# Opening of a two-layer decoder trunk: first transfers on two queues, written order of the first splits, two accumulations interleaved, one spread placed

## The chip, the cores and the metric

The kernel runs on one core of one Trainium2 chip, as a single program. The metric is the device time of that program in microseconds (us); the time of a kernel is the median of its runs.

The core has five engines that matter here. TensorE (PE in the profile) multiplies matrices into PSUM; VectorE (DVE), ScalarE (ACT) and GpSimd (POOL) work elementwise; SyncE (SP) issues transfers, and ScalarE can issue transfers too. Each engine executes its own instructions strictly in the order in which they stand in its queue. The transfers themselves run on 16 DMA engines.

## The reference

The input is one sequence of 512 tokens with 1024 features, in float32. Two layers follow one another; each has a mixer (layer 0 a causal Conformer convolution module, layer 1 differential attention), a SwiGLU feed-forward part and a gated per-layer embedding. The change touches only the beginning of layer 0:

```python
u = rms_norm(h, conv_norm_g)            # h = x
a = u @ w_pw1 + b_pw1                   # 1024 -> 2048
u = a[..., :D] * sigmoid(a[..., D:])    # gated half
u = depthwise_conv(u, 31 taps) + dw_b
u = silu(layer_norm(u))
h = h + (u @ w_pw2 + b_pw2)
```

`rms_norm` multiplies each token by one over the root of the mean of its squares, and each feature by a gain.

## The kernel before

**Layout.** Features lie on the 128 partitions and tokens along the free axis, so h is eight chunks h[0] to h[7] of 128 x 512. The weight w_pw1 comes in tiles of 128 x 1024, one for each 128 output features: its eight blocks of 128 x 128 are the stationary operands for the eight chunks of the input.

**Products in three parts.** Float32 products are made of three faster ones. Each operand is split into a high part, rounded to the type fp32r, and a low part, what the rounding left. For a weight, ScalarE casts the high part (L159) and VectorE subtracts (L161). For a chunk of the norm, `Norm.split` has ScalarE multiply h[c] by the gain and round (L206), and VectorE form the low part (L207). The gain is a column of a small table `vec`, which is loaded by a transfer of its own (L120). `mm3` then issues low x high (L166), high x high (L167) and high x low (L168). The text calls each of these 128x512 instructions a product.

**The norm is applied late.** The per-token factor is not applied to the input. It is worked out beside the products and multiplied into their result. `columns_of_chunks` squares every h chunk on ScalarE (L237); the squares of chunks 0 to 2 go one by one into a sum over features on TensorE (`columns_sum`, L199, short passes of 128 columns against a matrix of ones), those of chunks 3 to 7 are first added on GpSimd (L241) and then summed. VectorE (L270) and GpSimd (L272) make the inverse root, VectorE spreads it on a diagonal (L277), and `spread` multiplies this by ones on TensorE (L288), so that every partition holds the factor of every token. ScalarE copies that to SBUF as `rb` (L262).

**The conv stage.** The loop over c (L500) makes output chunk c: `half(wg)` and `half(wa)`, 24 products each (eight input chunks times three), fill two PSUM tiles; VectorE multiplies both by `rb` (L523, L529), ScalarE takes the sigmoid (L524), VectorE multiplies the two (L533 or L541). The convolution of a finished chunk is done in one of two ways. For chunks 0, 2, 4 and 7 most taps are run on VectorE (L453 to L458) and some on ScalarE and GpSimd (L445, L446); chunk 7 also has eight on TensorE (L363). The chunks in `PHASED` (1, 3, 5, 6) go through DRAM and come back in another layout (`phased_in`, L370 and L374), are convolved on TensorE with banded matrices (L407), and go back the same way (L417, L420). Weights of chunk c + 1 are loaded and split while chunk c is made, in two raw buffers (tag `wraw`): a load waits until the raw tile two loads ahead of it has been split.

**What sets the order.** The Tile framework's planner simulates the kernel when it is built and writes each engine's queue. It prefers what stands earlier in the program among the instructions that its simulation finds ready. `tc.issue_after(x)` adds an edge: what is issued in the block stands behind x on its engine. `tc.manual_schedule(engines=...)` keeps the written order on the named engines.

**The opening before.** SP issues the two halves of the first weight, h[0], the halves of the second weight, and the other chunks of h, in an order that alternates between them (L155, L297); ScalarE's queue issues `vec` alone. Nine warm-up products (`WARM`, L141) run on TensorE while the first transfers are under way. The planner chooses the order of casts, scalings and squares.

Of the kernel before, what the change touches and what calls it, by code (L numbers as in the profile page):

```python
# [13 lines left out]
F32R = mybir.dt.float32r  # L14
AF = mybir.ActivationFunctionType
ALU = mybir.AluOpType
# [4 lines left out]
P = 128  # L21
S = 512
D = 1024
NC = D // P
# [22 lines left out]


SHIFT = 1
WARM = 9  # L50
ALONE = (7,)
CUTS = 2

# [38 lines left out]
def trunk(ctx, tc, xT, pT, wts, diag, dww, vec, rel, onehot, lamv, out):  # L92
    nc = tc.nc
# [8 lines left out]
    def sb(shape, tag, bufs, dt=F32):  # L102
        uid[0] += 1
        return pool.tile(shape, dt, tag=tag, name=f"{tag}_{uid[0]}", bufs=bufs)
# [12 lines left out]


    vt = sb([P, 480], "vec", 1)[:, :NV]
    nc.scalar.dma_start(vt, vec)  # L120

    def col(name, i=0):
        a, _ = VEC[name]
# [5 lines left out]
    ones = f(ones_r)  # L129
# [2 lines left out]
    V.memset(mhalf, -0.5)  # L132
    V.memset(meps, DH * EPS)
    t = wk()[:, 0:P]
    V.memset(t, 1.0)
    V.tensor_copy(ones_r, t)

# [9 lines left out]
    def weight(n=1024, pieces=1, between=(), eng=V, after=(None, None), home=None, parts=None, bufs=1):  # L147
        i = wnext[0]
        wnext[0] += 1
        raw = sb([P, 1024], *(home or ("wraw", 2)))  # L150
        hi = sb([P, 1024], *((parts[0], bufs) if parts else ("whi", 4)), F32R)
        lo = sb([P, 1024], *((parts[1], bufs) if parts else ("wlo", 4)), F32R)
        for k in range(pieces):
            cut = slice(k * n // pieces, (k + 1) * n // pieces)
            loaded[0] = nc.sync.dma_start(raw[:, cut], wts[i, :, cut])  # L155
            if k < len(between):
                between[k]()
            with tc.issue_after(after[1].ins) if after[1] else nullcontext():
                A.copy(hi[:, cut], raw[:, cut])  # L159
            with tc.issue_after(after[0].ins) if after[0] else nullcontext():  # L160
                eng.tensor_tensor(lo[:, cut], raw[:, cut], f(hi[:, cut]), ALU.subtract)  # L161
        return hi, lo

    def mm3(acc, a, b, first, last, **kw):
        (ah, al), (bh, bl) = a, b
        T.matmul(acc, al, bh, start=first, stop=False, **kw)  # L166
        T.matmul(acc, ah, bh, start=False, stop=False, **kw)  # L167
        return T.matmul(acc, ah, bl, start=False, stop=last, **kw)  # L168
# [15 lines left out]
    def wpart(w, k):  # L184
        return tuple(
            t[k // 4][:, (k % 4) * P : (k % 4 + 1) * P] if isinstance(t, list) else t[:, k * P : (k + 1) * P] for t in w
        )
# [2 lines left out]
        return t[:, 0], t[:, 1]  # L190


    h = [sb([P, S], f"h{c}", 1) for c in range(NC)]

    def columns_sum(t, src, first, last):

        for b in range(4):
            cut = slice(b * P, (b + 1) * P)
            r = T.matmul(t[:, cut], src[:, cut], ones, start=first and b == 0, stop=last and b == 3)  # L199
        return r  # L200
# [8 lines left out]
    class Norm:  # L209
# [18 lines left out]
                self.square = A.activation(sq, h[c], AF.Square)  # L228
                self.last = self.eng.tensor_tensor(self.acc, self.acc, sq, ALU.add)  # L229

        def columns_of_chunks(self, n):

            t = tp()
            acc = sb([P, S], "acc", 1)
            for c in range(NC):
                sq = wk() if c != n else acc
                A.activation(sq, h[c], AF.Square)  # L237
                if c < n:
                    columns_sum(t, sq, c == 0, False)
                elif c > n:  # L240
                    G.tensor_tensor(acc, acc, sq, ALU.add)  # L241
            columns_sum(t, acc, False, True)
            return rsqrt_cols(first_of(t), 4, 1.0 / D)

        def columns(self):
# [5 lines left out]
        def diagonal(self):  # L251
            r = self.columns()
            rh = sb([P, P // 2], "r8", 2, F32R)[:, :4]
            rl = sb([P, P // 2], "v8", 2)[:, :4]
            V.tensor_copy(rh, r)
            V.tensor_tensor(rl, r, f(rh), ALU.subtract)
            self.dg = diagonal(f(rh), F32R), diagonal(rl, F32R)
# [17 lines left out]
    def diagonal(r, dt=F32):  # L275
# [6 lines left out]
        )  # L282
        return dg

    def spread(dg):
        t = tp()
        if not isinstance(dg, tuple):
            T.matmul(t, ones, dg, start=True, stop=True)  # L288
            return t
        for i, d in enumerate(dg):  # L290
            T.matmul(t, ones_r, d, start=i == 0, stop=i == 1)
        return t


    norm = Norm("conv_g")
    def load(c):
        return lambda: nc.sync.dma_start(h[c], xT[c])  # L297

    w0 = weight(pieces=2, between=(load(0),))
    norm.split(0)  # L300
    w1 = weight(pieces=2, between=(load(1), load(2)))
    pair_loads = [loaded[0]]
    pairs = [(w1, w0)]
    for c in range(3, NC):
        load(c)()
    for c in range(1, NC):
        norm.split(c)

    def pfeatures(layer, parts):
        for k, (hi, lo) in enumerate(parts):  # L310
# [26 lines left out]
    last_sum = [None]  # L337
    rb = None

    def half(w):  # L340
        acc = mm()
        for k in range(NC):
            mm3(acc, wpart(w, k), norm.u[k], k == 0, k == NC - 1)
        return acc

    def wt(c, j):
# [153 lines left out]
    for c in range(NC):  # L500
        wa, wg = pairs[c]
        if c == 0:
            pg = half(wg)
            pa = half(wa)
            norm.dg = diagonal(norm.columns_of_chunks(3))
            rb = norm.rows()
        if c + 1 < NC:
            pairs.append((weight(), weight())[::-1])
            pair_loads.append(loaded[0])
        if c == 0:  # L510
            dwt = sb([P, NC * KW], "C4", 2)
            nc.sync.dma_start(dwt, dww)
        if c == 1:
            ph = pfeatures(0, [(sb([P, S], t, 2, F32R), sb([P, S], t, 2, F32R)) for t in ("wth", "wtl")])
        if c > 0:
            pg = half(wg)
            for k in BETWEEN[c]:
                pe_taps(k)
            pa = half(wa)
            for k in BEHIND[c]:  # L520
                pe_taps(k)
        tg, ta = big(), big()
        V.tensor_tensor(tg, pg, rb, ALU.mult)  # L523
        gated = A.activation(tg, tg, AF.Sigmoid, bias=col("b_pw1", 8 + c))  # L524
        if c == NC - 1:

            with tc.issue_after(gated.ins):
                A.activation(powers[:, 24:32], vt[:, :8], AF.Silu)
        V.tensor_tensor(ta, pa, rb, ALU.mult)  # L529
        if c in PHASED:  # L530
            up = big()
            phases, tok = "p (r n) -> p n r", "p (n r) -> p n r"
            V.scalar_tensor_tensor(  # L533
                up.rearrange(phases, r=NPH), ta.rearrange(tok, r=NPH), col("b_pw1", c),
                tg.rearrange(tok, r=NPH), ALU.add, ALU.mult,
            )
            phased_in(c, up)
        else:
            up = ups[c] = sb([P, S + PAD], "C0", 2)
            G.memset(up[:, :PAD], 0.0)  # L540
            V.scalar_tensor_tensor(up[:, PAD:], ta, col("b_pw1", c), tg, ALU.add, ALU.mult)  # L541
        for k in BETWEEN[c] + BEHIND[c]:
            other_taps(k)
        if c == 1:
            moments(0)
        elif c > 3:
            moments(c - 3)
# [862 lines left out]
```

## Time and profile before

| | |
|---|---|
| median of 3 runs | 1245.88 us (1245.82 to 1248.12) |
| the profiled execution's own time | 1246.42 us |
| its span | 1244.7 us |
| busy: PE, DVE, ACT, POOL | 1232.4, 882.1, 623.8, 471.1 us |
| granted clock of TensorE | 1.00 |
| moved by DMA | 136.33 MB, mean 110 GB/s |

The profile comes from one execution. A row of the timeline gives the start, the duration, the engine, the line of the kernel, the operation, the tile written and the tiles read; in brackets stands how long the engine was idle before and what it waited for. PE rows are matmuls, PEld their weight loads; SPq and ACTq are the engines' issues of transfers. A row of busy time by stage gives the stage, its length, and then for PE, PEld, DVE, ACT and POOL the busy time with the number of instructions, the granted clock, the share of the DMA engines and the rate in GB/s; where it was asked for one engine, only that engine stands there.

### The profile page before, as it was taken

What the parts mean: (1) busy time and instruction counts of PE and PEld (TensorE: products, weight loads), DVE (VectorE), ACT (ScalarE), POOL (GpSimd) and SP (SyncE); (2) the same over time, 40 slices, a digit from 0 to 9 for tenths busy, and PEclk for the clock granted to TensorE, in tenths of its full rate; (3) what the DMA queues carried; (4) which work ended last, traced back from release to release, by engine and by line L of the source; (5) the groups of instructions that cost most, each with busy time, mean ns of one, the idle gap of its engine ahead of it and who ended that gap; (6) DMA issues with size and microseconds to landing.
All of it is one profiled execution on the core that took longest, in us unless ns stands there. A gap on an engine that the chain in (4) does not pass through costs nothing.

```text
span 1244.7 us, 18430 instructions
## 1 busy us (share of the span) xinstructions
PE 1232.4 (99%) x7080; PEld 1080.8 (87%) x7080; DVE 882.1 (71%) x1242; ACT 623.8 (50%) x1096; POOL 471.1 (38%) x355
## 2 busy tenths in 40 slices
PE   9999999999999999999999999999999999999998
PEld 7888788888998899888888888788889998999887
DVE  6998866885895479547676876646966885587535
ACT  5653464443553255434566877735434552455432
POOL 3863442024670364133346645041026650552120
PEclk9999999999999999999999999999999999999999
DMA  7566213334233322334332331143333333232331
GB/s 267 177 210 193 90 51 119 98 98 127 86 102 118 102 86 71 117 104 149 126 113 76 112 90 38 52 144 93 89 122 95 103 111 112 83 102 86 104 100 67
DMA packets 49154, 136.33 MB, mean 110 GB/s; under 512 B 5635, under 2 KB 10243, under 8 KB 49068
## 3 DMA queue, kind: packets, MB, share of 16 engines
q1 hardware_dynamic: 46944, 131.74, 34.0%
q10 hardware_dynamic: 2124, 3.43, 0.9%
q8 instruction: 55, 0.90, 0.3%
q14 instruction: 31, 0.25, 0.1%
HBM read 128.84 MB, written 6.31 MB: 109 GB/s over the span
## 4 chain that ended last, share of the span: by engine, by line
PE 88%; DVE 4%; issue 2%; DMA 1%; ACT 0%; SPq 0%; POOL 0%; DVEq 0%; ACTq 0%
PE mm L166 27%; PE mm L167 27%; PE mm L168 27%; PE mm L1126 1%; DVE sc L458 1%; PE sc L1094 1%; PE sc L1093 1%; PE tp L1113 1%; PE sc L407 1%; PE mm L407 1%; PE tp L1047 1%; PE mm L363 1%; PE tp L199 1%; DVE wlo L720 0%; DVE wlo L161 0%
## 5 line engine op out<-in xcount | busy, mean ns | idle before, releaser
L159 ACT CAST whi<-wraw 128x1024 fp32r<-128x1024 f32 (+2 forms) x145 | 145.7, 1014 | 229.0 <-PE mm L168 110.9
L161 DVE TENSOR_TENSOR wlo<-wraw,whi 128x1024 fp32r<-128x1024 f32 (+2 forms) x141 | 180.4, 1285 | 82.0 <-ACT whi L159 79.7
L166 PE MATMUL mm<-A,wlo 128*128 128x512 f32 (+1 forms) x568 | 220.4, 388 | 1.1 <-ACT A L206 1.0
L167 PE MATMUL mm<-A,whi 128*128 128x512 f32 (+1 forms) x568 | 219.2, 387 | 0.0
L168 PE MATMUL mm<-A,whi 128*128 128x512 f32 (+1 forms) x568 | 217.3, 389 | 0.0
L166 PE MATMUL mm<-B,wlo 128*128 128x512 f32 x352 | 137.0, 389 | 0.0
L167 PE MATMUL mm<-B,whi 128*128 128x512 f32 x352 | 137.0, 389 | 0.0
L168 PE MATMUL mm<-B,whi 128*128 128x512 f32 x352 | 135.6, 389 | 0.0
L229 POOL TENSOR_TENSOR acc<-acc,wk 128x512 f32<-128x512 f32 x35 | 60.0, 1715 | 190.6 <-ACT wk L228 189.9
L166 PEld LDWEIGHTS mm<-A,wlo 128*128 128x128 f32 x568 | 106.8, 188 | 23.7 <-ACT A L206 1.3
L167 PE MATMUL mm<-C,whi 128*128 128x256 f32 x448 | 126.8, 283 | 0.0
L168 PE MATMUL mm<-C,whi 128*128 128x256 f32 x448 | 126.8, 283 | 0.0
L166 PE MATMUL mm<-C,wlo 128*128 128x256 f32 x448 | 126.8, 283 | 0.0
L168 PEld LDWEIGHTS mm<-A,whi 128*128 128x128 f32 x568 | 106.5, 188 | 21.9 <-issue 0.5
L167 PEld LDWEIGHTS mm<-A,whi 128*128 128x128 f32 x568 | 106.7, 188 | 21.1
L720 DVE TENSOR_TENSOR wlo<-A,whi 128x1024 fp32r<-128x1024 f32 x60 | 106.2, 1778 | 19.7 <-ACT whi L719 19.6
L719 ACT CAST whi<-A 128x1024 fp32r<-128x1024 f32 x60 | 62.9, 1049 | 55.5 <-PE mm L168 44.3
L729 POOL TENSOR_TENSOR A<-A 128x512 f32<-128x512 f32 x16 | 25.7, 1606 | 165.5 <-DMA A<-in_wts 156.7
L729 POOL TENSOR_TENSOR A<-wraw 128x512 f32<-128x512 f32 x16 | 24.7, 1546 | 167.4 <-DMA wraw<-in_wts 152.7
L167 PEld LDWEIGHTS mm<-C,whi 128*128 128x128 f32 x448 | 86.0, 192 | 0.2
L166 PEld LDWEIGHTS mm<-C,wlo 128*128 128x128 f32 x448 | 86.0, 192 | 0.2
L168 PEld LDWEIGHTS mm<-C,whi 128*128 128x128 f32 x448 | 86.0, 192 | 0.0
(314 smaller groups left out, 3031.6 us busy)
## 6 DMA issues: line engine op xcount, KB each, us to landing
wraw<-in_wts SPq DMA_DIRECT2D x161, 512.0 KB, 3.6
A<-in_wts SPq DMA_DIRECT2D x32, 512.0 KB, 3.6
wraw<-in_wts SPq DMA_DIRECT2D x16, 384.0 KB, 3.1
D<-in_diag SPq DMA_DIRECT2D x22, 256.0 KB, 4.8
C<-in_diag SPq DMA_DIRECT2D x16, 256.0 KB, 4.8
h<-in_xT SPq DMA_DIRECT2D x8, 256.0 KB, 5.5
rest<-h SPq DMA_DIRECT2D x8, 256.0 KB, 2.5
bias<-scr ACTq DMA_DIRECT2D x8, 256.0 KB, 3.6
```

The lines of the kernel that those rows point to most:

```text
L159: A.copy(hi[:, cut], raw[:, cut])
L161: eng.tensor_tensor(lo[:, cut], raw[:, cut], f(hi[:, cut]), ALU.subtract)
L166: T.matmul(acc, al, bh, start=first, stop=False, **kw)
L167: T.matmul(acc, ah, bh, start=False, stop=False, **kw)
L168: return T.matmul(acc, ah, bl, start=False, stop=last, **kw)
L199: r = T.matmul(t[:, cut], src[:, cut], ones, start=first and b == 0, stop=last and b == 3)
L229: self.last = self.eng.tensor_tensor(self.acc, self.acc, sq, ALU.add)
L363: last_tap[0] = T.matmul(acc, dg[:, j % 4], ups[c][:, j : j + S], start=(j == 0), stop=(j == PE_TAPS[c] - 1))
L407: last_tap[0] = T.matmul(acc[:, g * P : (g + 1) * P], w, ups[c][:, g, LEAD - m : LEAD - m + P], start=(m == 0), stop=(m == LAGS - 1),)
L719: A.copy(hi, src)
L720: V.tensor_tensor(lo, src, f(hi), ALU.subtract)
L729: G.tensor_tensor(s[:, 0], r1[:, 0], r1[:, 1], ALU.add)
```

## The change

It has four parts, all in the opening.

1. **Transfers.** ScalarE's queue issues h[0], `vec` and h[1], in this order. SP issues the first weight in three pieces (columns 0 to 255, 256 to 511, 512 to 1023) and the second in two, with h[2] and h[3] between, and the other chunks of h behind them.
2. **Order.** The casts and low parts of these weight pieces, the splits of all chunks of h and all squares stand in a written order on ScalarE and VectorE. Chunk 3's square is the tile into which GpSimd adds those of chunks 4 to 7; the square of chunk 2 comes last.
3. **Chunk 0 of the output.** Both halves are issued together, chunk of the input by chunk; for the second half the order of the three products is high x high, high x low, low x high.
4. **The spread.** In the second half of output chunk 1, the products with input chunks 4 to 7 stand behind the first norm's spread. And there are eight warm-up products instead of nine.

The core of the diff:

```diff
-WARM = 9
+WARM = 8
...
-    nc.scalar.dma_start(vt, vec)
...
+    h = [sb([P, S], f"h{c}", 1) for c in range(NC)]
+    nc.scalar.dma_start(h[0], xT[0])
+    nc.scalar.dma_start(vt, vec)
+    nc.scalar.dma_start(h[1], xT[1])
...
+        def columns_of_chunks(self, squares):
             t = tp()
+            for c in range(4):
+                columns_sum(t, squares[c], c == 0, c == 3)
             return rsqrt_cols(first_of(t), 4, 1.0 / D)
...
+            last_spread[0] = T.matmul(t, ones, dg, start=True, stop=True)
...
+    pieces = (slice(0, 256), slice(256, S), slice(S, 1024)), (slice(0, S), slice(S, 1024))
...
-    w0 = weight(pieces=2, between=(load(0),))
-    norm.split(0)
-    w1 = weight(pieces=2, between=(load(1), load(2)))
...
+    fetch(0, 0)
+    fetch(1, 0)
+    fetch(0, 1)
+    load(2)
+    load(3)
+    fetch(0, 2)
+    pair_loads = [fetch(1, 1)]
     pairs = [(w1, w0)]
+    for c in range(4, NC):
+        load(c)
...
+    def square(c):
+        sq = squares[c] = wk() if c != 3 else sb([P, S], "acc", 1)
+        A.activation(sq, h[c], AF.Square)
+        if c > 3:
+            G.tensor_tensor(squares[3], squares[3], sq, ALU.add)
+
+    def first_split(i, k):
+        hi, lo = (w0, w1)[i]
+        cut = pieces[i][k]
+        A.copy(hi[:, cut], raw2[i][:, cut])
+        V.tensor_tensor(lo[:, cut], raw2[i][:, cut], f(hi[:, cut]), ALU.subtract)
+
+    with tc.manual_schedule(engines={V.engine, A.engine}):
+        first_split(0, 0)
+        norm.split(0)
+        first_split(1, 0)
+        norm.split(1)
+        first_split(0, 1)
+        square(0)
+        norm.split(2)
+        norm.split(3)
+        first_split(0, 2)
+        first_split(1, 1)
+        square(1)
+        norm.split(4)
+        square(3)
+        for c in (5, 6, 7):
+            norm.split(c)
+            square(c - 1)
+        square(7)
+        square(2)
...
-    def half(w):
+    def half(w, behind=None):
         acc = mm()
         for k in range(NC):
-            mm3(acc, wpart(w, k), norm.u[k], k == 0, k == NC - 1)
+            with tc.issue_after(behind.ins) if behind and k > 3 else nullcontext():
+                mm3(acc, wpart(w, k), norm.u[k], k == 0, k == NC - 1)
         return acc
...
         if c == 0:
-            pg = half(wg)
-            pa = half(wa)
-            norm.dg = diagonal(norm.columns_of_chunks(3))
+            pg, pa = mm(), mm()
+            for k in range(NC):
+                mm3(pg, wpart(wg, k), norm.u[k], k == 0, k == NC - 1)
+                (ah, al), (bh, bl) = wpart(wa, k), norm.u[k]
+                T.matmul(pa, ah, bh, start=k == 0, stop=False)
+                T.matmul(pa, ah, bl, start=False, stop=False)
+                T.matmul(pa, al, bh, start=False, stop=k == NC - 1)
+            norm.dg = diagonal(norm.columns_of_chunks(squares))
...
-            pa = half(wa)
+            pa = half(wa, last_spread[0] if c == 1 else None)
```

More of the change, by code (lines that the diff above doesn't have):

```diff
@@ L190, in both @@
         return t[:, 0], t[:, 1]
-    h = [sb([P, S], f"h{c}", 1) for c in range(NC)]
     def columns_sum(t, src, first, last):
@@ L229, in chunk @@
                 self.last = self.eng.tensor_tensor(self.acc, self.acc, sq, ALU.add)
-        def columns_of_chunks(self, n):
+        def columns_of_chunks(self, squares):
             t = tp()
[L234 to L242, printed above, removed]
+            for c in range(4):
+                columns_sum(t, squares[c], c == 0, c == 3)
             return rsqrt_cols(first_of(t), 4, 1.0 / D)
@@ L283, in diagonal @@
         return dg
+    last_spread = [None]
     def spread(dg):
@@ L287, in spread @@
         if not isinstance(dg, tuple):
-            T.matmul(t, ones, dg, start=True, stop=True)
+            last_spread[0] = T.matmul(t, ones, dg, start=True, stop=True)
             return t
@@ L295, in trunk, with fetch @@
     norm = Norm("conv_g")
+    wnext[0] = 2
+    raw2 = [sb([P, 1024], "wraw", 2) for _ in range(2)]
+    w0, w1 = ([sb([P, 1024], t, 4, F32R) for t in ("whi", "wlo")] for _ in range(2))
+    pieces = (slice(0, 256), slice(256, S), slice(S, 1024)), (slice(0, S), slice(S, 1024))
     def load(c):
-        return lambda: nc.sync.dma_start(h[c], xT[c])
-    w0 = weight(pieces=2, between=(load(0),))
-    norm.split(0)
-    w1 = weight(pieces=2, between=(load(1), load(2)))
-    pair_loads = [loaded[0]]
-    pairs = [(w1, w0)]
[L304 to L307, printed above, removed]
+        nc.sync.dma_start(h[c], xT[c])
+    def fetch(i, k):
+        return nc.sync.dma_start(raw2[i][:, pieces[i][k]], wts[i, :, pieces[i][k]])
+    fetch(0, 0)
[5 more added lines that the diff above has]
+    pair_loads = [fetch(1, 1)]
+    pairs = [(w1, w0)]
+    for c in range(4, NC):
+        load(c)
+    squares = {}
+    def square(c):
[27 more added lines that the diff above has]
+        square(2)
     def pfeatures(layer, parts):
```

## The prediction

> **What bounds the kernel now.** I read the head of the page first, then busy time by stage, to see where TensorE (PE) has room at all.
>
> ```profile
> span 1244.7 us, 18430 instructions
> ```
>
> ```profile
> 0.00:20.00 20.00, 17.53 (x87) 15.19 (x88) 13.68 (x19) 14.73 (x23) 7.18 (x14) 1.00 0.92 337
> 100.00:120.00 20.00, 18.26 (x117) 16.22 (x116) 17.98 (x23) 3.46 (x5) 2.55 (x3) 1.00 0.72 206
> 780.00:800.00 20.00, 18.48 (x108) 15.46 (x107) 15.64 (x49) 16.16 (x50) 2.33 (x4) 1.00 0.18 54
> 0.00:1240.00 1240.00, 1232.21 (x7080) 1080.85 (x7080) 880.82 (x1239) 623.35 (x1095) 471.06 (x355) 1.00 0.35 110
> ```
>
> The first pair of numbers in a row is the stage and its length, the next PE's busy time. PE is busy 1232.21 of 1240 us: 7.79 us idle in all, of which 2.47 in the first 20 us and 1.74 near 107 us. No product is removed, so these two places are nearly all that the change can reach. What happens before the first product of chunk 0 is in the timeline:
>
> ```profile
> 0.73 0.38 SPq L155 DMA_DIRECT2D wraw<-in_wts  x1
> 0.73 0.41 ACTq L120 DMA_DIRECT2D vec<-in_vec  x1
> 1.17 0.42 SPq L297 DMA_DIRECT2D h<-in_xT  x1
> 1.18 1.28 ACT L159 ACT_TABLE_LOAD   x1 [1.18 <-PEq L1399]
> 1.52 4.21 PE L141 MATMUL tp<-ones,ident 128*128 128x128 f32 x18 [1.52 <-POOL ident masks.py:199]
> 4.20 0.15 DVE L985 TENSOR_SCALAR mhalf<-vec 128x1 f32<-128x1 f32 x1 [2.89 <-DMA vec<-in_vec]
> 4.77 0.72 ACT L206 ACTIVATE A<-h,vec 128x512 fp32r<-128x512 f32 x1
> 5.53 0.75 DVE L207 SCALAR_TENSOR_TENSOR A<-h,vec,A 128x512 fp32r<-128x512 f32 x1 [0.16 <-ACT A L206]
> 5.55 0.58 PE L166 MATMUL mm<-A,wlo 128*128 128x512 f32 x1
> 6.56 0.69 DVE L161 TENSOR_TENSOR wlo<-wraw,whi 128x512 fp32r<-128x512 f32 x1 [0.28 <-ACT whi L159]
> ```
>
> The first product (5.55) starts when the first chunk of h has been scaled (4.77 plus 0.72). Then PE starves until the second chunk is split at 8.44, and is dense from there. Three stages and the products in them:
>
> ```profile
> 5.55:8.44 2.89, 1.94 (x13) 1.48 (x12) 2.13 (x4) 2.37 (x5) 0.00 (x0) 1.00 1.01 368
> 8.44:21.44 13.00, 13.00 (x70) 11.15 (x70) 11.58 (x10) 9.69 (x16) 6.21 (x4) 1.00 0.91 351
> 21.44:28.15 6.71, 6.71 (x33) 5.53 (x32) 3.44 (x5) 2.11 (x2) 1.03 (x1) 1.00 0.55 187
> ```
>
> ```profile
> L166 PE MATMUL mm<-A,wlo 128*128 128x512 f32 x10 | 4.0, 400 | 0.0
> ```
>
> This group, of the last stage alone, has 10 products; L167 has 10 and L168 has 9 beside it. So from 21.44 to 28.15 stand 29 products of chunk 1, and one takes 6.71/29 = 0.23 us. Chunk 0 has 48 products and 32 short passes of the sums of squares; three products and 8 passes lie before 8.44, so 45 and 24 fill 13.00 us: a pass takes (13.00 - 45 x 0.23)/24 = 0.11 us. The 2.89 us hold 3 x 0.23 + 8 x 0.11 = 1.57 us of such work. **1.3 us are lost** there, more than the busy time shows, since it counts a waiting or half-rate matmul as busy.
>
> The second place needs the next rows: the norm's spread, its copy rb, and what waits on them.
>
> ```profile
> 23.02 0.69 DVE L277 TENSOR_TENSOR wk<-ident,r 128x512 f32<-128x512 f32 x1 [1.14 <-POOL r L272]
> 28.15 1.02 PE L288 MATMUL tp<-wk,ones 128*128 128x512 f32 x2
> 29.46 0.58 ACT L262 COPY rb<-tp 128x512 f32<-128x512 f32 x1
> 30.07 0.69 DVE L523 TENSOR_TENSOR big<-mm,rb 128x512 f32<-128x512 f32 x1 [2.27 <-ACT rb L262]
> ```
>
> ```profile
> 30.07:64.47 34.40, 34.40 (x190) 29.84 (x189) 32.60 (x38) 23.81 (x33) 28.01 (x20) 1.00 0.59 184
> 64.47:98.86 34.39, 34.39 (x187) 29.47 (x187) 32.96 (x40) 16.25 (x24) 22.89 (x19) 1.00 0.54 184
> ```
>
> ```profile
> 107.58 4.26 PE L407 MATMUL sc<-C,D 128*128 128x128 f32 x36 [1.74 <-DMA C<-pi]
> ```
>
> The diagonal is ready at 23.71, but the spread stands behind 29 products in PE's queue and starts 4.4 us later. VectorE (third busy number) waits 2.27 us for rb, then works 32.60 of 34.40 and 32.96 of 34.39 us. The chain of waits runs along VectorE from 64.47 (its first traced step) to 98.86, then over the phased copy's DMA to 107.58, where PE has waited 1.74 us. So up to 107 us **VectorE sets the end, and PE has 1.74 us to spare**. PE work that is earlier by itself would only lengthen that wait. The saving is the smaller of two numbers: how much earlier rb comes, and how much earlier PE runs plus 1.74.
>
> **The change part by part.** *One warm-up product fewer* removes two of the 18 passes (L141), about 4.21/18 x 2 = 0.47 us, which end at 5.26 instead of just ahead of 5.55. The first product waits for the scaled chunk, so this is worth nothing on the path; what it may cost is a rival below.
>
> *First transfers.* Landings as the transfer view has them (last number: us from issue to landing):
>
> ```profile
> wraw<-in_wts SPq DMA_DIRECT2D x1, 256.0 KB, 3.3
> h<-in_xT SPq DMA_DIRECT2D x1, 256.0 KB, 3.5
> vec<-in_vec ACTq DMA_DIRECT2D x1, 49.5 KB, 3.4
> ```
>
> Now the weight lands at 4.03, vec at 4.13, h0 at 4.67. After, h0 is issued first on ScalarE's queue at 0.73, so by its own 3.5 it lands at 4.23, 0.44 earlier. But the scaling needs vec too, now issued second, at about 1.14: by its own 3.4 it lands at 4.54 (lower end). The upper end: h0 lands 0.64 behind a weight piece of the same 256 KB; if the queues take turns packet by packet, 256 KB of h0 and 256 KB of SP's next piece go ahead of vec where none did and 128 KB of the first piece less, 384 KB or 0.96 us behind 4.13: 5.09. I take the middle, 4.8, against 4.77 now: **no gain at the first product** (-0.2 to +0.3), because what h0 wins, vec loses. The short first piece lands sooner but waits for the same scaling; VectorE's wait for vec (L985) grows with it and holds only that piece's low part. The two more issues on ScalarE (0.41 each) push its table load from 1.18 to about 2.0, done at 3.3, before anything lands; SP issues 11 transfers where it had 12, so its later ones go out no later.
>
> The rows show both queues served in one stretch, 2.5 to 3.0 us:
>
> ```profile
> q1 hardware_dynamic: 43, 0.08, 57.7%
> q10 hardware_dynamic: 50, 0.02, 30.2%
> ```
>
> The Trainium skill, DMA: Bandwidth & Descriptors, section Issuing engines are not separate DMA queues, says that transfers begun by different engines interleave on the same 16 DMA engines, so a second queue saves only the time of issuing; 43 and 50 packets in one half microsecond agree. Taken strictly it puts vec at the upper end, and the sum below would be 0.3 us less gain.
>
> *Order of splits and squares, chunks interleaved.* ScalarE's steps follow each other by 0.61 us after a scaling (11.60 to 12.21) and 0.52 after a square (15.62 to 16.14, in the second fence below), from
>
> ```profile
> 11.60 0.71 ACT L206 ACTIVATE A<-h,vec 128x512 fp32r<-128x512 f32 x1
> 12.21 0.62 ACT L237 ACTIVATE wk<-h 128x512 f32<-128x512 f32 x1
> 12.91 6.44 POOL L241 TENSOR_TENSOR acc<-acc,wk 128x512 f32<-128x512 f32 x4 [11.38 <-ACT wk L237]
> ```
>
> From 4.8: scaling of chunk 0, cast of the second weight's half (as a square), scaling of chunk 1 from about 5.95, or when h1 lands. h1 is third on its queue: 3.5 after its issue at about 1.55 is 5.05, and by bytes (562 KB ahead of its end there, as much on SP, less the 306 KB that had landed by 4.13, at 0.64 us per 256 KB) 4.13 + 2.05 = 6.2; I take 6.1. Chunk 1 is then scaled at 6.8. On VectorE the low part of chunk 0 ends near 6.3 (5.53 + 0.75) and that of the weight 0.69 later, so the six products with chunk 0 end near 7.2: 1.65 us for 6 x 0.23 = 1.38, 0.3 lost; chunk 1's low part at 7.7 is in time. So **1.3 lost becomes 0.3, a gain of 1.0** (0 if the wait only moves, 1.3 if all goes; with the start, 0 to 1.5). The rows show PE already running both halves mixed, since the planner did so; writing the mix is worth nothing by itself.
>
> What could be late next is POOL's sum of five squares. The square that starts it stands 14 steps behind the start, six scalings and 7.5 of the others: 6 x 0.61 + 7.5 x 0.52 = 7.6, with 0.15 for h1 12.6, and 6.44 of additions end at 19.0. PE's other work for chunk 0 ends at 21.44 - 1.0 - 8 x 0.11 = 19.6, so 0.6 us cover it. The next weight load waits on SP for the first weight's raw buffer, whose last piece is now split near 10.2 (transfers are 0.64 apart), where the load went out at 7.72. The longest landing of an h chunk, 5.9 (last row below), would have it at 16.1, when ScalarE comes free of squares (15.62 + 0.52). Cast and low part then end near 18.9, and PE wants them at 20.4. 1.5 us of cover; without it each 1 us costs 1.
>
> ```profile
> 7.72 0.33 SPq L155 DMA_DIRECT2D wraw<-in_wts  x1
> 15.62 0.61 ACT L237 ACTIVATE wk<-h 128x512 f32<-128x512 f32 x1
> 16.14 1.98 ACT L159 CAST whi<-wraw 128x1024 fp32r<-128x1024 f32 x2
> 18.13 3.44 DVE L161 TENSOR_TENSOR wlo<-wraw,whi 128x1024 fp32r<-128x1024 f32 x2
> ```
>
> ```profile
> DMA to landing us min/median/max: 3.5/5.5/5.9
> ```
>
> *The spread's place.* The new edge forbids the last 12 products of chunk 1's second half ahead of the spread: a bound from above at 24 + 12 = 36 products, not a place. Chunk 0 ends at 20.4. Early end: at once when the diagonal is ready, 20.4 + 2.27 = 22.7, 5.4 earlier than now. Late end: 36 x 0.23 = 8.3 behind, 28.7, 0.6 later than now. I take the trace's own distance, 6.71, as what lies between the last sum of squares and the spread is the same chain: 27.1, **1.0 earlier**.
>
> *Sum.* rb 1.0 us earlier, PE 1.0 earlier: the wait at 107 us stays 1.74 and everything behind moves by 1.0; 0.1 off for the start's uneven ends, 0.9. The profiled execution took 1246.42 us (1244.7 of span), so 1245.5; the median shown is 1245.88, 0.54 below it, so the prediction on that scale is **1245.0**.
>
> **Rivals.** *The spread comes early.* If the planner, with a shorter chunk 0, issues it at least 1.74 us nearer to the diagonal, VectorE restarts at 27.3 or before and the wait at 107 goes: 0.9 + 1.74 = 2.6, 1243.3. For it: VectorE idles 2.27 us and has taps of chunk 0 to fill in; the diagonal waits 4.4 us. Against: nothing in the change pulls the spread forward.
>
> *The spread sits at its bound (slower).* At 36 products it starts near 28.7, rb is 0.6 later, the wait at 107 becomes 1.74 + 1.0 + 0.6, and the end moves by 0.6: 1246.5. It decides once the spread starts after 28.15. For it: earlier chunk-1 products can slip ahead of POOL's late sum, whose cover is 0.6 us. Against: the planner's present place is 29.
>
> *The clock is cold at the first products.* The warm-up passes follow each other by about 0.22 us and the passes at 6.20, eight in 1.05, by half that, while the granted clock reads 1.00 throughout.
>
> ```profile
> 6.20 1.05 PE L199 MATMUL tp<-ones,wk 128*128 128x128 f32 x8
> ```
>
> With one warm-up less and a gap before 5.55, the full rate may come a few us later: 12 products at twice 0.23 cost 2.8 us less the 0.3 lost anyway; 2.5 - 0.9 = 1.6 slower, 1247.5. Against: PE is still fed for 3.7 us. The Trainium skill, TensorE: Matmul & The Clock Gate, section Part 1: The HAM clock gate, says that the clock rises only after a busy window of about 3.4 us, that the windows run free of the kernel; the halved spacing fits, the clock column does not show it.
>
> *It isn't what it says.* A planner orders everything else, and a shifted start may reorder later stages. The waits there are small (1.52 us at 780 to 800); doubled or removed, some 3 us to either side.
>
> **How the numbers follow.** About 0.2%, 2.5 us, is what a measurement can tell from no change. Forecast 0.44 (own range 1244.2 to 1246.0); early spread 0.30, of which 0.23 past 2.5 us, since PE's own gain need only be 0.8; spread at its bound 0.10; cold clock 0.04; reordered elsewhere 0.12, split evenly. Faster: 0.23 and 0.06, 0.29. Slower: 0.06 for reordering, 0.06 where a bound spread or a cold clock meets another loss: 0.12. The rest, 0.59, is the same. Range 1242.3 to 1247.6: down to the early spread with the whole 1.5 on PE (3.2 in all) and 0.4 of reordering, up to the cold clock.
>
> **What would show it.** Right: the first product near 5.5, dense products from about 7.2, chunk 1's first product near 20.4, the spread near 27.1, the wait before L407 still near 1.7. Wrong: vec landing before 4.5; a spread before 25.4 or after 28.15; no wait at 107; first products 0.4 apart.

## The result, and the profile after

The changed kernel takes 1249.59 us (median of 9 runs, 1248.57 to 1251.66) against 1246.40 for the kernel before (9 runs, 1245.46 to 1248.12, beside it on the same chip). The ratio is 1.0028, with a 95% interval of 1.0017 to 1.0038. The change costs 3.2 us; 1245.0 was predicted, in a range that ended at 1247.6. The profiled execution took 1249.59 us, with this span:

```profile
span 1247.5 us, 18428 instructions
```

Busy time by stage of the changed kernel, columns as before. PE is 0.37 us less busy than before in the first 20 us, and 0.98 less near 107 us:

```profile
0.00:20.00 20.00, 17.16 (x76) 14.76 (x77) 13.34 (x21) 14.62 (x24) 7.05 (x14) 1.00 0.85 293
100.00:120.00 20.00, 17.28 (x114) 15.37 (x113) 18.02 (x21) 3.94 (x5) 4.91 (x4) 1.00 0.57 152
```

**The opening.** The transfer view of the changed kernel gives the landings (last number), and its timeline what waits for them. The row of h is h1, third on ScalarE's queue; the trace has no landing of h0:

```profile
wraw<-in_wts SPq DMA_DIRECT2D x1, 128.0 KB, 3.5
vec<-in_vec ACTq DMA_DIRECT2D x1, 49.5 KB, 4.6
h<-in_xT ACTq DMA_DIRECT2D x1, 256.0 KB, 4.9
```

```profile
1.17 0.45 ACTq L136 DMA_DIRECT2D vec<-in_vec  x1
4.29 0.40 ACT L325 CAST whi<-wraw 128x256 fp32r<-128x256 f32 x1 [0.88 <-DMA wraw<-in_wts]
5.85 0.72 ACT L207 ACTIVATE A<-h,vec 128x512 fp32r<-128x512 f32 x1 [1.16 <-DMA vec<-in_vec]
6.63 0.80 PE L169 MATMUL mm<-A,wlo 128*128 128x512 f32 x1 [1.33 <-ACT A L207]
7.22 0.63 PE L170 MATMUL mm<-A,whi 128*128 128x512 f32 x1
7.65 0.63 PE L547 MATMUL mm<-A,whi 128*128 128x512 f32 x1
...
9.78 0.47 PE L549 MATMUL mm<-A,wlo 128*128 128x512 f32 x1
10.09 0.39 PE L547 MATMUL mm<-A,whi 128*128 128x512 f32 x1
```

`vec`, now the second transfer on ScalarE's queue, lands 4.6 us after its issue at 1.17, where it took 3.4 as the first. The first scaling starts at 5.85 (4.77 before), the first product at 6.63 (5.55). The next products do not wait, yet they start 0.43 us apart, twice the 0.23 of the later ones, up to 9.78.

**The norm's factor.** The chain from the last sum of squares to VectorE's restart:

```profile
13.68 6.97 POOL L320 TENSOR_TENSOR acc<-acc,wk 128x512 f32<-128x512 f32 x4 [12.15 <-ACT wk L318]
21.78 0.48 PE L169 MATMUL mm<-A,wlo 128*128 128x512 f32 x1
...
23.02 1.05 PE L200 MATMUL tp<-ones,acc 128*128 128x128 f32 x8
30.14 0.62 ACT L352 CAST wth<-wraw 128x512 fp32r<-128x512 f32 x1 [2.57 <-DMA wraw<-in_pT]
30.50 1.02 PE L284 MATMUL tp<-wk,ones 128*128 128x512 f32 x2
31.73 0.62 ACT L352 CAST wtl<-wraw 128x512 fp32r<-128x512 f32 x1 [0.97 <-DMA wraw<-in_pT]
32.25 0.58 ACT L256 COPY rb<-tp 128x512 f32<-128x512 f32 x1
32.87 0.69 DVE L568 TENSOR_TENSOR big<-mm,rb 128x512 f32<-128x512 f32 x1 [4.04 <-ACT rb L256]
```

Chunk 1's first product starts at 21.78. GpSimd's sum is ready at 20.65 (13.68 + 6.97), but in PE's queue five products of chunk 1 stand ahead of the passes that sum it up (21.78 to 23.02). The spread comes at 30.50, 2.35 later than before. And rb's copy stands on ScalarE behind both casts of a weight that is still being transferred, the second of which ends its wait at 31.73. In the kernel before only the first cast stood ahead of it. This is the same stretch of ScalarE there:

```profile
28.93 0.62 ACT L313 CAST wth<-wraw 128x512 fp32r<-128x512 f32 x1 [2.39 <-DMA wraw<-in_pT]
29.46 0.58 ACT L262 COPY rb<-tp 128x512 f32<-128x512 f32 x1
30.45 0.62 ACT L313 CAST wtl<-wraw 128x512 fp32r<-128x512 f32 x1 [0.41 <-DMA wraw<-in_pT]
```

VectorE restarts at 32.87, against 30.07: 2.8 us late, where 1.0 early was forecast. The spread makes 2.35 of it, the copy's place 0.44: the copy starts 0.73 us behind the end of the spread, 0.29 before.

**Where it reaches PE.** Two waits of the changed kernel, and one of the kernel before (the other was shown, 107.58 with 1.74):

```profile
50.90 4.18 PE L447 MATMUL sc<-C,D 128*128 128x128 f32 x36
110.01 4.26 PE L447 MATMUL sc<-C,D 128*128 128x128 f32 x36 [2.72 <-DMA C<-pi]
158.07 1.12 PE L643 MATMUL tp<-wk,ones 128*128 128x512 f32 x2 [1.19 <-ACT wk L640]
```

```profile
49.68 4.18 PE L407 MATMUL sc<-C,D 128*128 128x128 f32 x36
154.94 1.12 PE L598 MATMUL tp<-wk,ones 128*128 128x512 f32 x2 [0.69 <-ACT wk L595]
```

PE is 1.22 us late at 50 us (50.90 against 49.68), from the start and the slow products. The wait near 107 us has grown from 1.74 to 2.72, another 0.98. I read it as coming from rb: from 32.87 VectorE works without a wait until 77.25, and the transfer that takes a finished chunk to DRAM (`pi<-big`, on SP) goes out at 101.41, against 99.05 before. The wait ahead of the LayerNorm's spread has grown from 0.69 to 1.19. That is 2.7 of the 3.1 us by which PE is late at 158; the spans differ by 2.8.

### The profile page after: what moved, and what is told of

Its sections match the earlier page's. It is cut to its first block, busy times and chain, and to the rows that moved or that the text cites. A ratio compares the mean times of both kernels' runs of the same rounds, so it can differ in the third digit from the quotient of the medians.

```text
span 1247.5 us, 18428 instructions
## 1 busy us (share of the span) xinstructions
PE 1233.4 (99%) x7078; PEld 1081.7 (87%) x7078; DVE 880.6 (71%) x1243; ACT 624.2 (50%) x1097; POOL 469.9 (38%) x355
## 4 chain that ended last, share of the span: by engine, by line
PE 85%; DVE 5%; DMA 2%; issue 2%; ACT 1%; POOL 0%; SPq 0%; DVEq 0%; ACTq 0%
PE mm L169 27%; PE mm L170 26%; PE mm L171 26%; DVE sc L498 2%; PE mm L1171 1%; DVE wlo L164 1%; PE sc L1139 1%; PE sc L1138 1%; DMA wraw<-in_wts 1%; PE tp L1158 1%; DMA B<-po 1%; PE tp L1092 1%; DVE B L465 0%; DMA po<-big 0%; PE tp L200 0%
## 5 line engine op out<-in xcount | busy, mean ns | idle before, releaser
L162 ACT CAST whi<-wraw 128x1024 fp32r<-128x1024 f32 (+1 forms) x141 | 143.4, 1025 | 224.9 <-PE mm L171 112.3
L164 DVE TENSOR_TENSOR wlo<-wraw,whi 128x1024 fp32r<-128x1024 f32 (+1 forms) x137 | 179.2, 1314 | 78.4 <-ACT whi L162 77.9
L169 PE MATMUL mm<-A,wlo 128*128 128x512 f32 (+1 forms) x560 | 217.7, 389 | 1.4 <-ACT A L207 1.3
L170 PE MATMUL mm<-A,whi 128*128 128x512 f32 (+1 forms) x560 | 217.7, 389 | 0.0
L171 PE MATMUL mm<-A,whi 128*128 128x512 f32 (+1 forms) x560 | 213.7, 387 | 0.0
```

## The experiments

The theory after this reading: two things cost, the late start (the second queue, and products at half rate) and the late rb (the spread behind 34 products, the copy behind two casts). The rivals: the rest of the planner's order, which shifts in every variant, makes the difference; or nothing but the spread's place counts. All kernels below compute the whole result. With each edit the planner writes the later queues anew, so two kernels differ in more than the edit, and what an edit is worth has that in it. "VectorE" is the start of its first product with rb, "wait" PE's wait near 107 us, both from the profiled execution; the ratio is to the kernel before on the same chip. The rows are in order of VectorE. The intervals of warm11, one_queue_w9, rb_first and spread24 overlap with that of the changed kernel; those of one_queue_w9_rb and one_queue_w9_s24 do not overlap with that of one_queue_w9.

| kernel | VectorE | wait | median us | ratio [95%] |
|---|---|---|---|---|
| vec_first | 33.67 | 2.37 | 1251.10 | 1.0036 [1.0022, 1.0050] |
| warm11 | 32.98 | 1.16 | 1248.64 | 1.0013 [1.0004, 1.0022] |
| the changed kernel | 32.87 | 2.72 | 1249.59 | 1.0028 [1.0017, 1.0038] |
| one_queue_w9 | 32.12 | 0.49 | 1248.60 | 1.0021 [1.0012, 1.0029] |
| one_queue | 31.84 | 3.94 | 1249.90 | 1.0030 [1.0019, 1.0042] |
| two_queues_alone | 31.80 | 3.24 | 1249.53 | 1.0027 [1.0018, 1.0036] |
| rb_first | 30.94 | 1.79 | 1247.77 | 1.0012 [1.0003, 1.0020] |
| before_spread24 | 30.34 | 0.46 | 1246.70 | 1.0000 [0.9991, 1.0009] |
| the kernel before | 30.07 | 1.74 | 1245.89 to 1246.49 | 1 |
| one_queue_w9_rb | 29.63 | 0.46 | 1246.45 | 0.9999 [0.9990, 1.0008] |
| w9_s24 | 28.88 | 1.41 | 1246.72 | 1.0003 [0.9995, 1.0012] |
| spread24 | 28.59 | 2.12 | 1247.64 | 1.0009 [1.0000, 1.0019] |
| one_queue_w9_s24 | 28.14 | 1.25 | 1245.75 | 0.9997 [0.9988, 1.0007] |
| before_spread12 | 27.66 | 2.73 | 1247.84 | 1.0015 [1.0006, 1.0024] |

### The order on ScalarE's queue

vec_first, the changed kernel with `vec` ahead of h0:

```diff
-    nc.scalar.dma_start(h[0], xT[0])
     nc.scalar.dma_start(vt, vec)
+    nc.scalar.dma_start(h[0], xT[0])
     nc.scalar.dma_start(h[1], xT[1])
```

> The changed kernel with vec issued ahead of h[0] on ScalarE's queue; TensorE's queue is the same as in the changed kernel. Theory A (the late table vec is what moved the start; the rate of the first products is its consequence): vec lands near 4.2 us, the first scaling starts near 4.7, the first product near 5.5, the products after it reach 0.23 us spacing by 6.5, rb is 2 us earlier, 1247.5 us. Theory B (late vec and a clock that is cold on its own, because of one warm-up product less): the first product is at 5.5 but products stay 0.43 us apart until about 9, rb is 1 us earlier, 1248.6 us. Rival C (the opening does not set the end): 1249.6 us.

Its transfer view and timeline:

```profile
h<-in_xT ACTq DMA_DIRECT2D x1, 256.0 KB, 5.4
```

```profile
6.67 0.72 ACT L207 ACTIVATE A<-h,vec 128x512 fp32r<-128x512 f32 x1 [2.83 <-DMA h<-in_xT]
```

Now h0 is the second and lands 5.4 us after its issue; the first scaling comes at 6.67, later still, and the kernel takes 1251.10 us. The order within the queue is not the cause: whichever comes second there is late.

### One queue, and the two queues alone

one_queue is the changed kernel with h0 and h1 on SP's queue; one_queue_w9 has nine warm-ups besides:

```diff
-    nc.scalar.dma_start(h[0], xT[0])
     nc.scalar.dma_start(vt, vec)
-    nc.scalar.dma_start(h[1], xT[1])
...
     fetch(0, 0)
+    load(0)
     fetch(1, 0)
+    load(1)
     fetch(0, 1)
```

> The changed kernel with vec alone on ScalarE's queue and all of h on SP's (first weight piece, h[0], second weight's half, h[1], then as in the change); the written order of splits and squares, the mixed halves, eight warm-up products and the bounded spread stay. Theory D (two queues delay vec or h[0], whichever stands second on ScalarE's queue, and so the first scaling by 1.1 us, and the pause lets the clock start cold): first scaling at 4.4 to 4.7 instead of 5.85, first product near 5.3, 1.2 us or more back on PE and rb, 1247.3 us. Rival E (the written order costs by itself): 1249 us or more. If both count: between.

> one_queue with nine warm-up products. Theory D: the start is the same, the warm-up now reaches the first product, so the half-rate products that some executions have go: 0 to 1 us below one_queue, 1246.6 to 1247.3 us, and a narrower spread of times. Rival: the ninth product only delays the first product by up to 0.2 us, 1247.5 us.

two_queues_alone is the kernel before with nothing of the change but the three transfers on ScalarE's queue:

```diff
-    nc.scalar.dma_start(vt, vec)
...
+    nc.scalar.dma_start(h[0], xT[0])
+    nc.scalar.dma_start(vt, vec)
+    nc.scalar.dma_start(h[1], xT[1])
```

> The kernel before with only h[0], vec, h[1] on ScalarE's queue, and SP's transfers as before without those two. Theory D: vec lands near 5.6, the first scaling is 0.9 to 1.1 us late, 1247.5 us or more (the nine warm-up products end ahead of it, so the clock may be cold too, up to 1 us more). Rival: the first scaling's delay is filled later: 1246.5 us.

Timelines of one_queue, and then of two_queues_alone:

```profile
4.01 0.72 ACT L205 ACTIVATE A<-h,vec 128x512 fp32r<-128x512 f32 x1 [0.34 <-DMA h<-in_xT]
28.11 1.02 PE L282 MATMUL tp<-wk,ones 128*128 128x512 f32 x2
30.70 0.62 ACT L352 CAST wtl<-wraw 128x512 fp32r<-128x512 f32 x1 [0.97 <-DMA wraw<-in_pT]
31.23 0.58 ACT L254 COPY rb<-tp 128x512 f32<-128x512 f32 x1
109.42 5.88 PE L447 MATMUL sc<-C,D 128*128 128x128 f32 x36 [3.94 <-DMA C<-pi]
```

```profile
5.83 0.72 ACT L207 ACTIVATE A<-h,vec 128x512 fp32r<-128x512 f32 x1
```

With one queue the first scaling starts 1.84 us earlier than in the changed kernel (4.01) and the spread 2.4 earlier (28.11), and nothing is won: 1249.90. The spread is done near 29.1, but rb is copied at 31.23, behind the cast that waits for its transfer, and two thirds of what PE gained it waits away near 107 us, 3.94 in place of 2.72. Behind that wait the first 36 matmuls of the taps take 5.88 us in place of 4.26, since the granted clock falls there, to 0.53 in this stage (PE alone, its clock behind the count; 1.00 in the changed kernel):

```profile
112.00:114.00 2.00, 2.00 (x12) 0.53 0.26 97
```

So the start was not the whole cause; the cast ahead of rb had not been in the reading until this run. With nine warm-ups besides the kernel takes 1248.60; its spread is at 28.24, its copy of rb at 31.51, as late as in one_queue. The two queues alone delay the first scaling of the kernel before by 1.06 us (5.83 against 4.77), as in the changed kernel, and that kernel loses 3.4 us (0.0027 x 1246). It is not a clean price: the planner reorders PE there too, rb is late as well (31.18), and in the profiled execution the clock falls behind the wait near 107 us here too (5.78 us for the 36 matmuls).

### More warm-ups

warm11 is the changed kernel with eleven:

```diff
-WARM = 8
+WARM = 11
```

> The changed kernel with 11 warm-up products instead of 8, so that they end near the first product (6.6 us). Transfers as in the change, vec late. Theory A and B alike: products are 0.23 us apart from the first, PE gains up to 1.5 us by 9.8 us, rb 0.5 to 1.3 us earlier, 1248.3 to 1249 us. Rival C: 1249.6 us, with the same spacing as before or without effect on the end.

Timeline of warm11; the first product is as late as in the changed kernel, and the next start 0.23 us apart:

```profile
6.62 0.71 PE L169 MATMUL mm<-A,wlo 128*128 128x512 f32 x1
7.16 0.39 PE L170 MATMUL mm<-A,whi 128*128 128x512 f32 x1
7.39 0.39 PE L547 MATMUL mm<-A,whi 128*128 128x512 f32 x1
```

The time falls by 0.95 us, to 1248.64, though VectorE restarts no earlier. Seven products at half rate cost 7 x 0.20 = 1.4 us of PE. That about 1 us of it reaches the end without an earlier rb fits a theory in which PE's own delay counts too; it is not shown, since the later order differs and the two intervals overlap.

### The spread's place

spread24 puts all of chunk 1's second half behind the spread, so that only the first half's 24 products stand ahead of it:

```diff
-            with tc.issue_after(behind.ins) if behind and k > 3 else nullcontext():
+            with tc.issue_after(behind.ins) if behind else nullcontext():
```

> The changed kernel with all of the second half of output chunk 1 behind the spread (not only the products with chunks 4 to 7): the spread moves from 34 to 24 products into chunk 1, about 2.4 us earlier. If rb sets the end through VectorE (my theory): VectorE restarts 2.4 us earlier, the 2.7 us wait before the taps near 107 us falls to about 0.4, 1247.2 us. If PE or something else sets it: 1249.6 us.

before_spread12 and before_spread24 are the kernel before with the spread behind 12 and behind 24 products of chunk 1 (29 as it was), by the same edge: in the one on products 4 to 7 of the first half and all of the second, in the other on the second half alone:

```diff
-    def half(w):
+    def half(w, behind=None, first=3):
...
+            with tc.issue_after(behind.ins) if behind and k > first else nullcontext():
...
-            pg = half(wg)
+            pg = half(wg, last_spread[0] if c == 1 else None)
...
-            pa = half(wa)
+            pa = half(wa, last_spread[0] if c == 1 else None, -1)
```

The line of pg stands in before_spread12 alone.

> The kernel before with the spread placed behind 12 products of output chunk 1 instead of 29 (the rest of chunk 1 stands behind it). If rb sets the end: rb 3.9 us earlier, the 1.74 us wait near 107 us goes and PE is dense, 1244.7 us. If the spread's place is not what sets it: 1246.4 us.

> The kernel before with one edit: all of chunk 1's second half behind the spread, so that it stands behind 24 products of chunk 1 and not 29. Theory (VectorE from rb sets the end): spread near 27.0, rb near 28.1 in place of 29.46, time 1.0 to 1.3 below the kernel before: 1244.6 to 1245.2. Rival (as with 12 products, 1247.84: what is won at rb is lost in the order of the later transfers on SyncE's queue, where the wait before the phased taps near 107 us grows): rb as early, the time 1246 or above.

Timeline of before_spread12, and then of before_spread24:

```profile
27.66 0.69 DVE L526 TENSOR_TENSOR big<-mm,rb 128x512 f32<-128x512 f32 x1
108.11 4.26 PE L410 MATMUL sc<-C,D 128*128 128x128 f32 x36 [2.73 <-DMA C<-pi]
```

```profile
29.20 0.62 ACT L315 CAST wth<-wraw 128x512 fp32r<-128x512 f32 x1 [1.95 <-DMA wraw<-in_pT]
29.73 0.58 ACT L262 COPY rb<-tp 128x512 f32<-128x512 f32 x1
```

In the changed kernel the place is worth 2 us (1247.64). There the copy also comes ahead of both casts, and the lead can be followed: VectorE finishes the gated half of chunk 0 at 32.87 in place of 34.90, and the `pi<-big` near 100 us goes out at 99.43 in place of 101.41. But the first products of its profiled execution ran at full rate, so part of it may be PE's. In the kernel before it is worth nothing, for two reasons. With 12 products VectorE restarts 2.4 us earlier, and the kernel is 1.4 us slower (1247.84 against 1246.49 beside it): the wait near 107 us has grown to 2.73. VectorE's lead is gone by then: `pi<-big` goes out at 99.28, against 99.05. With 24 the spread ran at 27.24, 0.9 earlier, but rb did not follow: its copy (29.73) stands behind the first cast, which waits for its transfer until 29.20. The expectation had overlooked that the cast, not the spread, is what ends last there. As rb did not move, neither did the time.

### The copy's place on ScalarE

rb_first is the changed kernel with the copy of rb ahead of both casts; one_queue_w9_rb is one_queue_w9 with the same edit:

```diff
-            A.copy(r, spread(self.dg))
+            last_rb[0] = A.copy(r, spread(self.dg))
...
-            A.copy(hi, raw)
+            with tc.issue_after(last_rb[0].ins) if layer == 0 else nullcontext():
+                A.copy(hi, raw)
```

> The changed kernel with one edit: on ScalarE the copy rb of the spread stands ahead of the two casts of the phased weights (wth, wtl) that wait for their transfer; in the changed kernel it stands behind both (casts at 30.14 and 31.73, rb at 32.25, the spread's matmuls at 30.50 done near 31.5). TensorE's order is all but the same. Theory (VectorE from rb sets the end, and what the change lost at rb is lost at the end): rb near 31.5 and VectorE's product with it near 32.2, 0.7 us earlier; time 0.4 to 0.7 below the changed kernel's 1249.59: 1248.9 to 1249.2. Rival (rb's moment does not matter, the planner's order of later transfers does): no change at 1249.6, or a shift that has nothing to do with 0.7.

> The changed kernel with h0 and h1 back on SyncE's queue and 9 warm-ups (1248.60 measured), and with rb ahead of the casts wth and wtl on ScalarE. There the spread runs at 28.24 and rb's copy only at 31.51, behind wtl at 30.98 which waits for its transfer. Theory (VectorE from rb sets the end): rb near 29.3, 2.2 us earlier, as early as the kernel before has it (29.46), and with all else as before the time falls by most of it: 1246.4 to 1247.0. Rival (the gain of the kernel with the spread behind 24 products came from TensorE's order and not from rb): rb 2.2 earlier and the time still 1248.3 to 1248.9.

Timeline of one_queue_w9_rb:

```profile
27.96 1.02 PE L283 MATMUL tp<-wk,ones 128*128 128x512 f32 x2
29.01 0.59 ACT L254 COPY rb<-tp 128x512 f32<-128x512 f32 x1 [1.64 <-PE tp L283]
29.95 0.62 ACT L354 CAST wth<-wraw 128x512 fp32r<-128x512 f32 x1 [0.35 <-DMA wraw<-in_pT]
```

The spread is nearly where it was (27.96 against 28.24), the copy 2.5 us earlier, and the time falls from 1248.60 to 1246.45, by 2.15: the theory's number, and level with the kernel before. But the trace does not show the theory's path. The sigmoid still stands behind the cast wtl on ScalarE, and VectorE finishes the gated half of chunk 0 no earlier. Timeline of one_queue_w9_rb, and then of one_queue_w9:

```profile
34.18 0.75 DVE L588 SCALAR_TENSOR_TENSOR C<-big,vec,big 128x512 f32<-128x512 f32 x1 [2.66 <-ACT big L571]
```

```profile
34.16 0.75 DVE L586 SCALAR_TENSOR_TENSOR C<-big,vec,big 128x512 f32<-128x512 f32 x1 [0.15 <-ACT big L569]
```

So the lead of 2.5 us is gone at 34.2, in a second wait. What differs behind it is order: `pi<-big` near 100 us goes out at 98.34, against 102.70. PE's wait near 107 us is the same (0.46 against 0.49), that ahead of the LayerNorm shorter (0.69 against 1.18), and two of one_queue_w9, 1.39 at 134 us and 1.11 at 149, are gone. The profiled execution, 1244.90, is 1.55 below the median. The run shows that this edit wins 2.15 us with the first transfers unchanged; that it won them through VectorE's restart is not shown, and the agreement with the theory's number may be luck.

rb_first falls by 1.8, more than the 0.4 to 0.7 expected. Its profiled execution had its first products at full rate, so its spread was earlier as well (29.27). And with the new order both waits shrank, the one near 107 us from 2.72 to 1.79 and the LayerNorm's from 1.19 to 0.69. The copy starts 0.7 us closer to the spread; how much of the 1.8 that is worth is not separated.

### Together

one_queue_w9_s24 joins one queue, nine warm-ups and the spread behind 24 products; w9_s24 is the same with the two queues of the change. The orders of the two on PE, VectorE and ScalarE are nearly the same.

```diff
-WARM = 8
+WARM = 9
...
-            with tc.issue_after(behind.ins) if behind and k > 3 else nullcontext():
+            with tc.issue_after(behind.ins) if behind else nullcontext():
```

> one_queue_w9 with the spread behind 24 products of chunk 1. By spread24 this took 2.0 us off the changed kernel: 1245 us, below the kernel before. Rival: with PE early the late-spread loss is already gone, or PE and the SP queue set the end: 1246.5 us.

> The changed kernel with its two queues kept, 9 warm-ups and the spread behind 24 products of chunk 1; the orders of TensorE, VectorE and ScalarE are nearly those of the kernel with one queue, 9 warm-ups and 24 products (1245.75 measured), so the difference between the two is the first transfers alone. Theory (the second queue costs its 1.1 to 1.8 us of start whole, now that nothing later hides it): first scaling near 5.85 against 4.01, first product 6.6 against 5.4, time 1246.9 to 1247.3. Rival (the start is hidden behind VectorE's later waits): the first product as late, the time within 0.5 of 1245.75.

With the three repairs the changed kernel is at 1245.75, 0.9997 of the kernel before: no faster, within what is measured. With the two queues it is 1246.72. By the ratios the two queues cost 0.0006 x 1246 = 0.7 us, less than the 1.24 us by which the first product is late (6.61 against 5.37) and less than was expected. At the spread 0.60 of it is left (26.83 against 26.23), since the first three products of the kernel with one queue ran at half rate in its profiled execution; the intervals of the two overlap, so this term is the least certain one. No variant beat the kernel before by a measurable amount.

## Why the prediction was wrong

**The step that failed first: "vec lands at 4.8, no gain at the first product".** It landed at 5.8 (1.17 + 4.6), and the scaling started at 5.85. The upper end of the bounds, 5.09, reckoned with turns by bytes over the stretch to the first landings; the second transfer on ScalarE's queue took 4.6 us to land, 5.4 when it was h0. In the direction it was the right mechanism, turns between two queues; its size was off by 1 us. By the Trainium skill, DMA: Bandwidth & Descriptors, section Issuing engines are not separate DMA queues, a second issuing engine saves no more than issue time; these traces agree, and here it cost 1.1 us of start.

**"1.3 lost becomes 0.3, a gain of 1.0".** The interleaving did what was worked out: from 6.63 to 21.78 PE does not starve. 48 products and 24 passes at 0.23 and 0.11 us are 13.7 us, the stretch is 15.15, and the 1.5 over are the seven products at half rate. So the gain of 1.0 was eaten by the cold clock, which stood in the prediction as a rival of its own with a chance of 0.04. The pause ahead of the first product, 1.33 us where the kernel before shows none, is not the cause by itself: rb_first and spread24 paused longer (1.64 and 1.62) and ran at full rate at once, and one_queue_w9_s24 had three products at half rate with no pause. So this step stays open in its cause. Chunk 1's first product came at 21.78, not 20.4.

**"I take the trace's own distance, 6.71": the largest miss.** From chunk 1's first product to the spread it was 30.50 - 21.78 = 8.72 us. Ahead of the spread now stand 34 products, and the eight passes over GpSimd's sum, which had been ahead of chunk 1: 34 x 0.23 + 8 x 0.11 = 8.7. The rival "the spread sits at its bound" named this mechanism (products of chunk 1 slip ahead of the late sum) and the point from which it decides (28.15), and it is what happened, though not for the reason given: the sum was ready at 20.65, ahead of chunk 1's first product, and it was the planner's order that held its passes back. It priced rb 0.6 late, since it was worked out from an early chunk 0 and a copy that follows at once.

**What was not in it at all: rb's place on ScalarE.** The prediction followed the spread on PE's queue, and took for granted that its copy follows. In the rows of the kernel before the copy is already behind a cast that waits 2.39 us for a transfer, and its row names no wait for the spread. In the changed kernel it is behind two, which makes 0.44 us of rb's delay. In one_queue_w9 the spread is level with the kernel before (28.24), and the copy's place makes nearly all of the delay (31.51 against 29.46); with it moved, the time fell by 2.15 us, by a path that is not shown.

**"VectorE from rb sets the end", and the smaller of two numbers.** It fits on the side of a late rb, in the changed kernel and in spread24. It is not proven there: the chain of waits starts near 64 us in the kernel before and near 66 in the changed kernel, and does not reach back to rb. one_queue agrees in part: its PE was 1.9 us ahead of the changed kernel's near 50 us, 0.6 ahead once the wait near 107 was over, and 1.1 late at 159; the last loss of 1.7 is the clock's, 5.88 - 4.26 = 1.6. On the side of an early rb it fails, and with it the rival "the spread comes early" (1243.3): five variants restart VectorE 0.4 to 2.4 us earlier than the kernel before, and none is measurably faster. VectorE then waits a second time, for the sigmoid: 1.34 to 2.66 us in these five, 1.18 in the kernel before. The prediction held that the wait near 107 us would go. In before_spread12 it grew. These are VectorE's largest wait on the way there and the order of transfers on SP (its timeline, and then that of the kernel before):

```profile
62.59 0.69 DVE L484 SCALAR_TENSOR_TENSOR B<-tp,B 128x512 f32<-128x512 f32 x1 [2.30 <-ACT shrow L483]
101.80 0.86 SPq L423 DMA_DIRECT2D B<-po  x2
102.75 1.80 SPq L377 DMA_DIRECT2D C<-pi  x4
```

```profile
101.57 0.38 SPq L420 DMA_DIRECT2D B<-po  x1
102.04 1.80 SPq L374 DMA_DIRECT2D C<-pi  x4
```

One more transfer of finished taps (`B<-po`) stands ahead of those that PE waits for (`C<-pi`), which go out 0.71 us later; PE reaches the wait 0.46 earlier and waits 0.99 longer. That the wait at 62.59 and this order are why is argued from the traces; no run isolates it. The same holds for the LayerNorm's wait, 0.69 in some kernels and 1.19 in others.

**The sum.** Forecast: PE and rb 1.0 early, 0.9 won. Measured: PE 1.2 late at 50 us, rb 2.8 late, of which 1.0 shows in the wait near 107 us, and 0.5 in the LayerNorm's; 2.8 of span. What lies behind 158 us takes 1089.4 us (1247.5 - 158.07) against 1089.8 before (1244.7 - 154.94), so the rival of a reordering in later stages did not come. Two others, a cold clock and a late spread, came together with a late start. The prediction set 0.06 aside for one of the two meeting another loss, but its range ended at the cold clock alone, and the case of both was not priced.

## What to carry to other kernels

When a result passes through a copy on another engine, read what that engine holds ahead of the copy: an in-order engine that waits there for a transfer delays it, whatever was done for its producer. Where several losses can come together, as here a late start, slow first products and a late spread, price that case too. And an early restart is worth something only until the next wait: here that for the sigmoid, which stands behind a cast that waits for its transfer. When a variant hits the forecast time, check in its trace that the path is the forecast one.

## What the hardware showed that was not expected

**The second transfer of a queue.** With `vec` alone on ScalarE's queue, the first 128 KB piece of the weight landed 2.5 us after its issue, and h0 and h1, on SP's queue, 3.5 (median of the two; transfer view of one_queue):

```profile
h<-in_xT SPq DMA_DIRECT2D x2, 256.0 KB, 3.5
wraw<-in_wts SPq DMA_DIRECT2D x1, 128.0 KB, 2.5
```

With h0 ahead of `vec` on ScalarE's queue the same piece took 3.5 and `vec` 4.6, though it has only 49.5 KB. With `vec` ahead of h0 there, in vec_first, the piece took 2.5 again.

**The clock at the start.** After 3.8 us of warm-up and a pause of 1.33 us, the products ran at half rate for 3.15 us in the changed kernel's profiled execution, and at full rate at once in that of rb_first, with the same warm-up and a longer pause, 1.64:

```profile
6.82 0.50 PE L169 MATMUL mm<-A,wlo 128*128 128x512 f32 x1 [1.64 <-ACT A L207]
7.15 0.40 PE L170 MATMUL mm<-A,whi 128*128 128x512 f32 x1
```

In vec_first the first products started 0.24 to 0.33 us apart behind a pause of 2.16, and then at half rate from 8.56 to 12.11. So the length of the pause does not decide it in these executions.

The column by stage reads 1.00 through the changed kernel's opening, though its products start at half rate. It does read 0.50 in vec_first from 9 to 11 us, and it falls to 0.50 for about 3.4 us behind the wait near 107 us in one_queue, two_queues_alone and vec_first. Their waits were 3.94, 3.24 and 2.37; behind 2.72 in the changed kernel and 2.73 in before_spread12 it stays at 1.00. The price is the 36 matmuls at 5.78 to 5.88 us in place of 4.26, about 1.6 us.

From run to run the changed kernel took 1248.57 and 1248.78 us at a mean granted clock of 1.000, and 1250.63 to 1251.66 in the four executions at 0.998 and 0.997. Where those four lost their clock no trace shows; a stretch like that near 112 us lowers the mean by 3.4 x 0.5 / 1248 = 0.0014, an opening like the profiled one does not show in the column. The Trainium skill, TensorE: Matmul & The Clock Gate, section Part 1: The HAM clock gate, gives 427 ns from start to start for a cold product of 512 columns, and says that the gate watches windows of about 3.4 us that run free of the kernel; the 0.43 us and the 3.4 us here agree with it, and that the windows run free is not shown by these traces.
